# Thirteen output pairs of the input projection formed from seven block products, their weight sums on GpSimd, and the convolution's input moved through DRAM

## The chip, the core and the metric

The kernel runs on one core of a Trainium2 chip. A core has a matrix engine (TensorE, "PE" in the profile; the loading of its weights is "PEld"), a vector engine (VectorE, "DVE"), a scalar engine (ScalarE, "ACT"), a general engine (GpSimd, "POOL") and a queue engine (SyncE, "SP") that here only issues DMAs. Each engine executes its own instructions in the order in which they stand in its program, and waits on semaphores for the others. TensorE accumulates in PSUM, which GpSimd's operations in this kernel never touch; all else lies in SBUF or in DRAM.

The metric is the device time of one launch in microseconds (us): the median of several runs. Lower is better.

## The reference

The reference is one layer of a hybrid block on 1024 tokens of width 1024, all in float32. After an RMS norm, one wide projection gives the inputs of a gated unit (a convolution branch), of attention, and of two gates:

```python
h = rms_norm(x, norm1_g[l])
z = h @ w_in[l]
glu_in, q, k, v, gate_logits = jnp.split(z, SPLITS, axis=-1)
a_val, a_gate = jnp.split(glu_in, 2, axis=-1)
a = a_val * jax.nn.sigmoid(a_gate)
a = causal_depthwise_conv(a, conv_w[l], conv_b[l])      # 31 taps, each channel alone
a = jax.nn.silu(rms_norm(a, conv_norm_g[l]))
y_a = a @ w_conv_out[l]
...                                                     # dilated attention, 16 heads of 64 -> y_b
g_a, g_b = jnp.split(jax.nn.sigmoid(gate_logits + gate_b[l]), 2, axis=-1)
x = x + (g_a * y_a + g_b * y_b) @ w_out[l]
h = rms_norm(x, norm2_g[l])
u = causal_depthwise_conv(h @ w_up[l], ffn_conv_w[l], ffn_conv_b[l])
u_val, u_gate = jnp.split(u, 2, axis=-1)
x = x + (jax.nn.silu(u_gate) * u_val) @ w_down[l]       # d_ff 2816
```

The parts that this case is about are the four column groups of `z` called `a_val`, `a_gate`, `g_a` and `g_b`, each 1024 channels wide, and the 31-tap convolution.

## The kernel before, in words

**Precision.** A float32 product is made from three products of shortened numbers: every operand is split into a high part (rounded by a ScalarE copy) and a low part (what is left, a VectorE subtraction), and high x high, high x low and low x high are summed in PSUM. So each block product stands as three matmuls of 128 x 128 by 128 x 512. The helper `split` (L76 to L79) does it; the weights go through `wsplit` and `wpiece`.

**First stage.** The 1024 x 1024 tokens are normed, turned by TensorE and kept in SBUF in two halves of 512 tokens, as high and low parts (`hT`). Then come, in program text, (1) the gated unit: for each of eight tiles of 128 channels a gate product and a value product (`gemm_ch`, L115, 48 matmuls each), a sigmoid on ScalarE, a multiplication on VectorE (L445) whose result goes into one of ten padded SBUF rows `apad`; (2) the projections q, k and v, six groups of eight token tiles (`gemm_tok`, L120, 24 matmuls each); (3) the convolution (`conv_branch`, L450): 31 VectorE operations over 128 x 1024 for each of eight channel tiles, from `apad` to `cacc`. No table sets the order of this stage: a scheduler places the instructions of each engine from its own estimate of time. It starts the convolution as soon as the first channel tile exists, two channel tiles in turn, and lets it fill VectorE all through the stage. VectorE's other work (low parts, norms of q and k) is placed between.

**Attention.** Sixteen heads, each in eight slots. Here the order of PE, DVE and ACT is written out by hand (`manual_schedule`): scores, a VectorE minimum and mask (L592), an exponential on ScalarE (L597), a scaling of the row on GpSimd (L601), transposes (L607), a split into high and low parts, and the weighted sum. Between these, TensorE is given side work in steps of three matmuls: the sixteen gate tiles and the eight tiles of `w_conv_out` (`side_steps`), of which `FILL` says how many steps each of the eight slots takes, and `COVER` how many are done before attention starts, while the convolution is normed. VectorE forms the low parts of that side work in L163.

**Rest.** Output projections and merging, then the up projection of the feed-forward part, whose value and gate tiles are already formed together from seven block products instead of eight (`product`, L846, with the weight sums on VectorE), then the down projection.

## Time and profile before

| | |
|---|---|
| time, median of 3 runs | 1762.45 us (1762.37 to 1762.9) |
| span of the profiled execution, first to last instruction | 1761.6 us, 0.85 us under that median |
| busy: PE, PEld | 1749.1 us, 1454.3 us |
| busy: DVE, ACT, POOL | 1329.3 us, 771.7 us, 185.9 us |
| first token tiles turned and split | 0 to about 42 us |
| gated unit's products | 41.6 to 193.9 us |
| q, k, v | 193.9 to 470.5 us |
| convolution on VectorE | 44.7 to 479.4 us |
| attention with side work | about 494 to 944 us |

The profile's own execution ran for a span of 1761.6 us; the page shows no other time for it. "Busy" is the time in which an engine had an instruction in work. A row of a group reads: line, engine, operation, output <- inputs, shapes, count, then busy time and the mean length of one, then the idle time just before them and what ended it. A row of a timeline reads: start, length, engine, line, operation, output <- inputs, and in brackets the idle time before it with its releaser. Lengths of neighbouring instructions on VectorE and TensorE overlap a little, since the next one starts before the last one has drained.

### The profile page before, as it was taken

How to read it: one execution, taken by the hardware profiler on the slowest of the kernel's cores; microseconds unless marked ns; L12 is line 12 of the kernel's file. 1: busy time of each engine (PE TensorE's matmuls, PEld its weight loads, DVE VectorE, ACT ScalarE, POOL GpSimd, SP SyncE). 2: the span in 40 equal slices, each digit the busy share in tenths (PEclk: the TensorE clock that was granted, in tenths of full speed). 3: DMA queues.
4: the chain of work that ended last, by engine and by line, in shares of the span. 5: the costliest groups of instructions: out<-in, count | busy, mean ns of one | idle time of the engine just before them, and what ended most of it. 6: DMA issues, size and time to landing. Idle time of an engine off the chain costs nothing.

```text
span 1761.6 us, 22662 instructions
## 1 busy us (share of the span) xinstructions
PE 1749.1 (99%) x8248; PEld 1454.3 (83%) x8248; DVE 1329.3 (75%) x1837; ACT 771.7 (44%) x1235; POOL 185.9 (11%) x193
## 2 busy tenths in 40 slices
PE   8999999999999999999999999999999999999999
PEld 6888888888888888888888888888888888888887
DVE  6999999999846666667655564687776777779863
ACT  6111132232256666667564343454544544534431
POOL 1000133034012222222210000000000000000000
PEclk9999999999999999999999999999999999999999
DMA  5111145344585655568446567532222222498851
GB/s 208 48 48 49 42 138 164 123 132 139 179 273 157 179 159 159 161 180 244 139 138 227 173 233 279 207 124 84 84 84 84 77 91 84 128 341 320 292 174 48
DMA packets 146530, 272.79 MB, mean 155 GB/s; under 512 B 11761, under 2 KB 61041, under 8 KB 146418
## 3 DMA queue, kind: packets, MB, share of 16 engines
q1 hardware_dynamic: 145264, 269.24, 47.2%
q10 hardware_dynamic: 1154, 2.10, 0.3%
q8 instruction: 65, 1.06, 0.2%
q14 instruction: 47, 0.39, 0.1%
HBM read 197.90 MB, written 73.40 MB: 154 GB/s over the span
## 4 chain that ended last, share of the span: by engine, by line
PE 93%; DMA 4%; DVE 1%; issue 1%; ACT 1%; SPq 0%; ACTq 0%; DVEq 0%
PE dx L1118 6%; PE xz L850 6%; PE xz L851 6%; PE xz L852 6%; PE qkv L129 5%; PE qkv L127 5%; PE qkv L128 5%; PE dy L1118 4%; PE pp L607 3%; PE gate L110 3%; PE gate L112 3%; PE gate L111 3%; PE y L850 2%; PE y L851 2%; PE y L852 2%; PE o L622 2%
## 5 line engine op out<-in xcount | busy, mean ns | idle before, releaser
L461 DVE SCALAR_TENSOR_TENSOR cacc<-apad,pk,cacc 128x1024 f32<-128x1024 f32 x240 | 299.7, 1288 | 0.7
L79 DVE TENSOR_TENSOR pl<-pp,ph 128x512 fp32r<-128x512 f32 x192 | 100.8, 553 | 88.1 <-ACT ph L78 87.9
L127 PE MATMUL qkv<-hi_qkv,hT 128*128 128x512 f32 x384 | 151.8, 396 | 0.0
L129 PE MATMUL qkv<-hi_qkv,hT 128*128 128x512 f32 x384 | 150.2, 391 | 0.0
L128 PE MATMUL qkv<-lo_qkv,hT 128*128 128x512 f32 x384 | 149.3, 389 | 0.0
L78 ACT ACTIVATE ph<-pp 128x512 fp32r<-128x512 f32 x192 | 87.1, 488 | 121.0 <-PE pp L607 120.3
L592 DVE CUSTOM_DVE_ANT_0 p<-s,m 128x128 f32<-128x128 f32 (+7 forms) x128 | 96.5, 754 | 53.3 <-PE s L588 41.4
L601 POOL TENSOR_SCALAR p<-p,st 128x128 f32<-128x128 f32 (+7 forms) x128 | 97.1, 758 | 315.7 <-DVE st L600 218.7
L1021 DVE SCALAR_TENSOR_TENSOR u<-u,pk 128x1023 f32<-128x1023 f32 x88 | 112.4, 1279 | 1.0 <-ACT u L1019 0.7
L103 POOL TENSOR_TENSOR rs<-ss,mhalf 128x8 f32<-128x8 f32 x32 | 75.0, 2348 | 337.6 <-DVE ss L102 337.6
L110 PE MATMUL gate<-hT,hi_gt 128*128 128x512 f32 x256 | 103.0, 402 | 0.0
L597 ACT ACTIVATE p<-p,st 128x128 f32<-128x128 f32 (+7 forms) x128 | 99.3, 775 | 5.5 <-DVE st L592 4.6
L111 PE MATMUL gate<-hT,hi_gt 128*128 128x512 f32 x256 | 100.3, 392 | 0.0
L112 PE MATMUL gate<-hT,lo_gt 128*128 128x512 f32 x256 | 100.1, 392 | 0.0
L129 PEld LDWEIGHTS qkv<-hi_qkv,hT 128*128 128x128 f32 x384 | 72.1, 188 | 15.3
L79 DVE TENSOR_TENSOR lo_uv<-raw_uv,hi_uv 128x1024 fp32r<-128x1024 f32 x20 | 24.5, 1226 | 79.5 <-ACT hi_uv L78 79.5
L128 PEld LDWEIGHTS qkv<-lo_qkv,hT 128*128 128x128 f32 x384 | 72.2, 188 | 14.3
L607 PE MATMUL pp<-ident,p 128*128 128x128 f32 x576 | 83.8, 272 | 0.0
L127 PEld LDWEIGHTS qkv<-hi_qkv,hT 128*128 128x128 f32 x384 | 72.2, 188 | 13.9
L607 PEld LDWEIGHTS pp<-ident,p 128*128 128x128 f32 x576 | 70.1, 140 | 15.3
L621 PE MATMUL o<-ph,v 128*128 128x512 f32 x192 | 74.8, 393 | 0.7 <-DVE op L633 0.7
L850 PE MATMUL xz<-blk_t,hi_s3g 128*128 128x512 f32 x176 | 68.6, 390 | 0.7 <-ACT xc L995 0.7
(309 smaller groups left out, 4638.8 us busy)
## 6 DMA issues: line engine op xcount, KB each, us to landing
wr<-w_down SPq DMA_DIRECT2D x45, 512.0 KB, 5.5
gr<-dff SPq DMA_DIRECT2D x62, 256.0 KB, 5.2
raw_qkv<-w_qkv SPq DMA_DIRECT2D x24, 512.0 KB, 3.8
dff<-u SPq DMA_DIRECT2D x22, 512.0 KB, 2.6
raw_uv<-w_up SPq DMA_DIRECT2D x21, 512.0 KB, 3.2
raw_ug<-w_up SPq DMA_DIRECT2D x20, 512.0 KB, 3.2
dv<-v SPq DMA_DIRECT2D x16, 512.0 KB, 3.2
raw_gt<-w_ch SPq DMA_DIRECT2D x16, 512.0 KB, 5.2
```

The source lines that it names most:

```text
L110: pe.matmul(o, hi[:, k, :], ah[:, k, :], start=(k == 0), stop=False)
L111: pe.matmul(o, hi[:, k, :], al[:, k, :], start=False, stop=False)
L112: pe.matmul(o, lo[:, k, :], ah[:, k, :], start=False, stop=(k == KT - 1))
L127: pe.matmul(ps, ah, hi[:, k % 2, :], start=(k == 0), stop=False)
L128: pe.matmul(ps, ah, lo[:, k % 2, :], start=False, stop=False)
L129: pe.matmul(ps, al, hi[:, k % 2, :], start=False, stop=(k == KT - 1))
L461: dve.scalar_tensor_tensor(out=acc, in0=a[:, j : j + T], scalar=w(j), in1=acc, op0=ALU.mult, op1=ALU.add)
L607: pe.transpose(pp[:, qb * P : (qb + 1) * P], pts[qb][:, kt * P : (kt + 1) * P], ident)
L850: pe.matmul(o, wh[:, k, :], bh[:, k, :], start=(start and k == 0), stop=False, skip_group_check=not start)
L851: pe.matmul(o, wh[:, k, :], bl[:, k, :], start=False, stop=False, skip_group_check=not start)
L852: end = pe.matmul(o, wl[:, k, :], bh[:, k, :], start=False, stop=(k == 3), skip_group_check=not start)
L1118: pe.matmul(banks[n], a[:, c], b[:, d], start=(start and i == 0 and m == 0), stop=(stop and i == nf - 1 and m == 2), skip_group_check=True)
```

## The change

The gated unit's tiles 1 to 7 and six of the eight gate pairs (`GATES = 6`: columns g_a and g_b of the same tile) are formed as *pairs*: the value tile and the gate tile together are a 2 x 2 block product over two halves of the input width and two halves of the tokens, and are made from seven block products of 12 matmuls (`product`, now ahead of the stage) instead of eight. For that the tokens are needed in four more forms (`t1` to `t4`: sums and differences of the blocks, each 128 x 2048, split into high and low), and each pair's weights in four sums.

- The sums of the weights (`add_`, L409, four of 128 x 512 for each of the 13 pairs) are done by GpSimd. So are two additions of 128 x 2048 (`rebuilt`, L477) that put the blocks of the first token half together again from high and low part.
- Each pair's weights are now three pieces of 1024 columns and one of 512 that are split, where two pieces of 1024 were; each pair has three additions of PSUM halves on VectorE (L552, L558, L560).
- The gated unit's result goes through DRAM (`dain`) instead of staying in `apad`: the convolution has two `apad` and two `cacc` buffers, loads its input, and stores its result (`dacc`), from where it is loaded again to be normed (L712).
- The block `b12` of the tokens is spilled to DRAM and fetched again for q, k and v, since its room holds the results of the pairs in between.
- The side work left for `COVER` and attention is four gate tiles (6, 7, 14, 15) and `w_conv_out`; `FILL` is about halved to go with it, `COVER` stays.

```diff
-FILL = (1.5, 3.4, 1.8, 1.9, 1.6, 3.0, 2.1, 2.2)
+FILL = (0.7, 1.6, 0.9, 0.9, 0.8, 1.5, 1.0, 1.1)
+GATES = 6
...
-        for c in range(12):
+        left_over = [c for c in range(16) if c % 8 >= GATES]
+        turn = left_over[-4:]
+        for c in left_over[:-4]:
...
+        def pair_sums(i, v):
+            n, c, _, w2 = pairs[i]
+            g = stage(w2, f"{n}g{c}")
+            s = wp.tile([P, 1024], F32, tag="raw", bufs=4, name=f"{n}s12_{c}")
+            a11, a12, a21, a22 = v[:, 0:512], v[:, 512:], g[:, 0:512], g[:, 512:]
+            s1, s2 = s[:, 0:512], s[:, 512:]
+            add_ = lambda o, a, b, op: pool.tensor_tensor(out=o, in0=a, in1=b, op=op)
+            add_(s1, a21, a22, ALU.add)
+            add_(s2, s1, a11, ALU.subtract)
+            sw = wsplit(s, f"{n}s12_{c}")
+            add_(a21, a11, a21, ALU.subtract)
+            gw = wsplit(g, f"{n}s3g_{c}")
+            add_(a12, a12, s2, ALU.subtract)
+            return [four(t) for t in sw], [four(t) for t in gw], [four(t) for t in wsplit(a12, f"{n}s4_{c}")]
...
+            def rebuilt(n, k):
+                pool.tensor_tensor(out=plain[n], in0=h0[0][:, k : k + 4].bitcast(F32),
+                                   in1=h0[1][:, k : k + 4].bitcast(F32), op=ALU.add)
+            rebuilt("t2", 0)
...
+        dve.tensor_tensor(out=plain["t2"], in0=plain["t3"], in1=plain["t2"], op=add)
+        dve.tensor_tensor(out=plain["t4"], in0=plain["t4"], in1=plain["t2"], op=sub)
+        for n in ("t2", "t1", "t3", "t4"):
+            forms[n] = tform(n)
+            split(forms[n][:, 0], forms[n][:, 1], plain[n])
...
+            put(uv[:, t0], X, 0)
+            dve.tensor_tensor(out=uv[:, t0], in0=Z, in1=uv[:, t0], op=add)
+            product(X, sh[:, 4:8], sl[:, 4:8], *fb["t2"], False)
+            put(uv[:, t1], X, 0)
+            product(Y, sh[:, 0:4], sl[:, 0:4], *fb["t1"], True)
+            put(p5, Y, 1)
+            product(X, gh[:, 0:4], gl[:, 0:4], *fb["t3"], False)
+            dve.tensor_tensor(out=ug[:, t1], in0=X, in1=p5, op=add)
+            product(Y, *s4, *fb["b22"], False)
+            dve.tensor_tensor(out=uv[:, t1], in0=Y, in1=uv[:, t1], op=add)
+            product(X, gh[:, 4:8], gl[:, 4:8], *fb["t4"], False)
+            put(ug[:, t0], X, 1)
+            if kind == "u":
+                act.activation(ug, ug, AF.Sigmoid)
+                dve.tensor_tensor(out=uv, in0=uv, in1=ug, op=ALU.mult)
+                sp.dma_start(dain[c], uv)
...
-            else:
-                gp = big_ps(f"glug_{c}")
-                gemm_ch(gp, wsecond[0] if c == 1 else wpiece(w_ch[8 + c], f"g{c}"), hT)
-                act.activation(sg, gp, AF.Sigmoid)
-                vp = big_ps(f"gluv_{c}")
-                gemm_ch(vp, wsecond[1] if c == 1 else wpiece(w_ch[c], f"v{c}"), hT)
-                dve.tensor_tensor(out=a[:, CW - 1 :], in0=vp, in1=sg, op=ALU.mult)
...
-                acc = p1.tile([P, CW - 1 + T], F32, tag="apad", bufs=10, name=f"cacc_{c}")[:, 0:T]
-                a = apad[c]
+                a = p1.tile([P, CW - 1 + T], F32, tag="apad", bufs=2, name=f"apad_{c}")
+                pool.memset(a[:, : CW - 1], 0.0)
+                sp.dma_start(a[:, CW - 1 :], dain[c])
+                acc = p1.tile([P, T], F32, tag="cacc", bufs=2, name=f"cacc_{c}")
...
+            sp.dma_start(ct, dacc[c])
             dve.tensor_tensor(out=ct, in0=ct, in1=sqacc, op=ALU.mult)
```

How the instructions stand now, at three places. First GpSimd's queue while the first tokens are normed (`st` is the statistic of one token tile, raised to the power -1/2 here; `mhalf` holds that exponent). Before:

```order
L103 TENSOR_TENSOR st_214<-st_214,mhalf 128x1
L431 MEMSET apad_829 128x30
L431 MEMSET apad_944 128x30
L103 TENSOR_TENSOR st_214<-st_214,mhalf 128x1
L431 MEMSET apad_1059 128x30
```

Now (`raw_uv` and `raw_ug` are the loaded weights of a pair, `us` its sums):

```order
L104 TENSOR_TENSOR st_226<-st_226,mhalf 128x1 x4
L477 TENSOR_TENSOR sums<-hT_220,hT_221 128x2048
L104 TENSOR_TENSOR st_226<-st_226,mhalf 128x1
L409 TENSOR_TENSOR us_1_590<-raw_ug_588 128x512
L409 TENSOR_TENSOR us_1_590<-us_1_590,raw_uv_408 128x512
L409 TENSOR_TENSOR raw_ug_588<-raw_uv_408,raw_ug_588 128x512
L104 TENSOR_TENSOR st_226<-st_226,mhalf 128x1 x3
L477 TENSOR_TENSOR t_sum<-hT_220,hT_221 128x2048
```

The statistics of token tiles 4 to 7 now stand behind one addition of 128 x 2048 and three of the first pair's sums.

Second, VectorE in the middle of the stage (`cacc` is the convolution's sum). Before, between two products of the gated unit:

```order
L461 SCALAR_TENSOR_TENSOR cacc_3502<-apad_496,pk,cacc_3502 128x1024
L445 TENSOR_TENSOR apad_714<-gluv_773,sg_716 128x1024
L461 SCALAR_TENSOR_TENSOR cacc_3469<-apad_489,pk,cacc_3469 128x1024
L79 TENSOR_TENSOR lo_v_1007<-raw_v_1004,hi_v_1006 128x1024
L461 SCALAR_TENSOR_TENSOR cacc_3502<-apad_496,pk,cacc_3502 128x1024
```

Now, between two pairs:

```order
L80 TENSOR_TENSOR lo_uv_1017<-raw_uv_1014,hi_uv_1016 128x1024
L603 SCALAR_TENSOR_TENSOR cacc_4299<-apad_4296,pk,cacc_4299 128x1024
L80 TENSOR_TENSOR lo_us_5_1051<-us_5_1047,hi_us_5_1050 128x1024
L603 SCALAR_TENSOR_TENSOR cacc_4336<-apad_4333,pk,cacc_4336 128x1024
L560 TENSOR_TENSOR uring<-uy_u_942,uring 128x512
L603 SCALAR_TENSOR_TENSOR cacc_4299<-apad_4296,pk,cacc_4299 128x1024
L80 TENSOR_TENSOR lo_us3g_1056<-raw_ug_1045,hi_us3g_1055 128x1024
L565 TENSOR_TENSOR uring<-uring 128x1024
L558 TENSOR_TENSOR uring<-uxz_898,up_u_943 128x512
```

Operations of the pair (low parts of weights, additions of PSUM halves) stand between single steps of the convolution, so each of them comes after those steps in VectorE's order.

Third, where the convolution ends on VectorE, seen from the last piece of the last weights of q, k and v (`lo_qkv_3`; `ql`, `qn` and `ss` belong to the norms of q and k, `v_0` is the first of the last eight token tiles, all of which need that piece). Before:

```order
L79 TENSOR_TENSOR lo_qkv_3_3081<-raw_qkv_3_3078,hi_qkv_3_3080 128x1024
L79 TENSOR_TENSOR ql_4_3010<-qt_4_3004,qh_4_3009 128x512
L461 SCALAR_TENSOR_TENSOR cacc_3712<-apad_1174,pk,cacc_3712 128x1024
L79 TENSOR_TENSOR ql_5_3055<-qt_5_3049,qh_5_3054 128x512
L461 SCALAR_TENSOR_TENSOR cacc_3677<-apad_1059,pk,cacc_3677 128x1024
L488 TENSOR_TENSOR qn_6_3002<-qkv_6_2970,rs_4_6_2997 128x512
L102 TENSOR_SCALAR ss_4_7_3041<-ss_4_7_3041 128x8
L461 SCALAR_TENSOR_TENSOR cacc_3712<-apad_1174,pk,cacc_3712 128x1024
```

Now:

```order
L80 TENSOR_TENSOR lo_qkv_3_3908<-raw_qkv_3_3905,hi_qkv_3_3907 128x1024
L80 TENSOR_TENSOR ql_5_3882<-qt_5_3876,qh_5_3881 128x512
L603 SCALAR_TENSOR_TENSOR cacc_4564<-apad_4561,pk,cacc_4564 128x1024
L103 TENSOR_SCALAR ss_4_7_3868<-ss_4_7_3868 128x8
L80 TENSOR_TENSOR ql_6_3946<-qt_6_3940,qh_6_3945 128x512
L603 SCALAR_TENSOR_TENSOR cacc_4564<-apad_4561,pk,cacc_4564 128x1024
L629 TENSOR_TENSOR qn_7_3874<-qkv_7_3842,rs_4_7_3869 128x512
L603 SCALAR_TENSOR_TENSOR cacc_4564<-apad_4561,pk,cacc_4564 128x1024
L80 TENSOR_TENSOR v_0_3936<-qkv_0_3911,v_0_3936 128x8x64
L610 TENSOR_TENSOR sqacc<-sqacc,apad_4561 128x1024
```

Before, 25 of the convolution's steps stood behind this weight piece, the last of them behind the eighth of these token tiles. Now three do, all ahead of the first tile. On TensorE 147 of the 192 matmuls of the last eight tiles stand from the first use of that piece on.

220 lines of the change are left out of this document (150 added, 70 removed).

## Prediction

> **What bounds the kernel now.** I read the page's busy times, its slices and the shares of the chain first, and then the busy times of two stretches: the gated unit with q, k, v (42 to 480 us) and eight heads of attention (535 to 735 us).
>
> ```profile
> PE 1749.1 (99%) x8248; PEld 1454.3 (83%) x8248; DVE 1329.3 (75%) x1837; ACT 771.7 (44%) x1235; POOL 185.9 (11%) x193
> DVE  6999999999846666667655564687776777779863
> PE 93%; DMA 4%; DVE 1%; issue 1%; ACT 1%; SPq 0%; ACTq 0%; DVEq 0%
> 42.00:480.00 438.00, 438.00 (x1994) 362.35 (x1994) 426.31 (x449) 101.81 (x139) 75.02 (x32) 1.00 0.34 106
> 535.00:735.00 200.00, 200.00 (x1103) 170.60 (x1101) 129.39 (x327) 123.59 (x277) 48.61 (x65) 1.00 0.59 165
> ```
>
> In the stretches the columns are the stretch, its sum, then busy time of PE, PEld, DVE, ACT and POOL, the granted clock, the DMA share and GB/s. TensorE never pauses in either, so fewer matmuls are time won, as long as the others keep up. The share of 75% for VectorE hides where that fails: in the first stretch, the one that the change rebuilds, VectorE is busy for 426.31 of 438 us. There two engines set the end together, and the question is on which side of that balance the change falls.
>
> **TensorE's gain.** A pair takes 84 matmuls where two tiles took 96, so 13 pairs save 156.
>
> ```profile
> L110 PE MATMUL glug<-hT,hi_g x112: 389/389/389, 41.6 to 182.4; 128*128 128x512 f32 x112
> L127 PE MATMUL qkv<-hi_qkv,hT x384: 387/389/481, 193.9 to 469.8; 128*128 128x512 f32 x192
> L129 PE MATMUL qkv<-hi_qkv,hT x384: 388/389/481, 194.4 to 470.2; 128*128 128x512 f32 x192
> ```
>
> The row of `glug` is one of six groups of 112 (three passes, gate and value): 672 matmuls from 41.6 to 193.9 us, 0.2266 us each. So 156 are worth **35.4 us**. The stage itself grows, since gate work moves into it from attention: 13 x 84 = 1092 matmuls stand where 672 were, 95.2 us more. Its last matmul ended near 470.5 us and would end at 565.7 us if TensorE never waited. Attention's side work shrinks by the other 130.6.
>
> **VectorE's own work.** The prices:
>
> ```profile
> L461 DVE SCALAR_TENSOR_TENSOR cacc<-apad,pk,cacc 128x1024 f32<-128x1024 f32 x240 | 299.7, 1288 | 0.7
> L445 DVE TENSOR_TENSOR apad<-gluv,sg 128x1024 f32<-128x1024 f32 x7 | 8.6, 1226 | 3.9 <-PE gluv L112 3.9
> L79 DVE TENSOR_TENSOR lo_v<-raw_v,hi_v 128x1024 fp32r<-128x1024 f32 x6 | 7.3, 1221 | 1.5 <-ACT hi_v L78 1.5
> L79 DVE TENSOR_TENSOR v<-qkv,v 128x512 fp32r<-128x512 f32 x16 | 10.9, 697 | 3.3 <-ACT v L78 3.1
> L163 DVE TENSOR_TENSOR lo_gt<-raw_gt,hi_gt 128x512 fp32r<-128x512 f32 x8 | 5.2, 687 | 0.0
> 209.03 1.22 DVE L469 TENSOR_TENSOR sqacc<-sqacc,csq 128x1024 f32<-128x1024 f32 x1
> 210.17 1.29 DVE L461 SCALAR_TENSOR_TENSOR cacc<-apad,pk,cacc 128x1024 f32<-128x1024 f32 x1
> 475.49 3.93 DVE L461 SCALAR_TENSOR_TENSOR cacc<-apad,pk,cacc 128x1024 f32<-128x1024 f32 x3
> ```
>
> Gone ahead of the convolution's last step: 14 low parts of gated weights (17.1 us), seven multiplications (8.6), ten low parts of gate weights (6.9) and seven splits of `v` that now stand behind it (4.9): 37.5 us. New: low parts for 13 pairs, three of 1024 and one of 512 columns (13 x 4.35 = 56.6); 39 additions from PSUM at 0.68 (26.5); seven multiplications (8.6); eight differences of token tiles at 0.69 (5.5); and six operations over 2048 columns. Those have no row; another 512 columns cost 1.226 - 0.687 = 0.54, so 2.3 each, 13.8. Together 111.0, the balance +73.5. Recorded lengths overlap: the operation at 209.03 is 1.22 long, but the next starts 1.14 later, so I count 0.934 of them, 68.6 us. The convolution's last step before ends at 479.4; it would end at **548.0**.
>
> That is under 565.7, but the end is not where TensorE needs VectorE. By the third place of the order the last weight piece of q, k, v stands only three convolution steps and three operations of 512 (5.5 us) ahead of it, so at 542.5; and 147 matmuls (33.3 us) wait for it, which have to start at 532.4 to end at 565.7. VectorE is **10.1 us** late there with nothing else counted. Before, the piece came just in time, with 25 steps still behind it.
>
> **The sums on GpSimd.** 52 additions of 128 x 512 at GpSimd look free: it is busy for 75.02 of 438 us. Attention shows that they may not be.
>
> ```profile
> L601 POOL TENSOR_SCALAR p<-p,st 128x1024 f32<-128x1024 f32 x16 | 18.1, 1129 | 11.9 <-DVE st L600 11.5 <-PE pp L607 0.4
> L601 POOL TENSOR_SCALAR p<-p,st 128x512 f32<-128x512 f32 x16 | 11.4, 715 | 49.3 <-PE pp L607 47.7 <-DVE st L600 1.6
> L601 POOL TENSOR_SCALAR p<-p,st 128x128 f32<-128x128 f32 x16 | 6.0, 375 | 34.0 <-DVE st L600 29.4 <-PE pp L607 4.5
> 559.63 0.69 DVE L163 TENSOR_TENSOR lo_gt<-raw_gt,hi_gt 128x512 fp32r<-128x512 f32 x1
> 577.84 1.42 DVE L163 TENSOR_TENSOR lo_gt<-raw_gt,hi_gt 128x512 fp32r<-128x512 f32 x1
> 577.71 1.02 POOL L601 TENSOR_SCALAR p<-p,st 128x896 f32<-128x896 f32 x1 [2.26 <-DVE st L600]
> 555.04 1.10 DVE L163 TENSOR_TENSOR lo_gt<-raw_gt,hi_gt 128x512 fp32r<-128x512 f32 x1
> 554.47 1.13 POOL L601 TENSOR_SCALAR p<-p,st 128x1024 f32<-128x1024 f32 x1 [0.92 <-DVE st L600]
> 209.21 5.02 POOL L103 TENSOR_TENSOR rs<-ss,mhalf 128x8 f32<-128x8 f32 x2 [182.35 <-DVE ss L102]
> ```
>
> The same subtraction takes 0.69 us alone, 1.42 when GpSimd has just begun (GpSimd ends at 578.73, the subtraction 0.53 later) and 1.10 in the middle (GpSimd ends at 555.60, the subtraction 0.54 later). So a VectorE operation that reads two tiles from SBUF waits until GpSimd's running instruction is over. Convolution steps and low parts all read two; the additions from PSUM read one. A power over 128 x 8 (209.21) held up no step beside it; it reads far less.
>
> GpSimd has no row for an addition of two 128 x 512 tiles. With one input it takes 0.715, the lower bound. The rows give 0.84 ns for an element and 0.27 fixed; if the second input streams as well, 0.27 + 2 x 0.43 = 1.13, near what 1024 elements take. Less 0.15 of start, in which nothing was held, that is 0.565 to 1.0 us of hold. I take 1.0: a sum does read two tiles. Additions from PSUM are 26.5 of the some 228 us of twelve pairs, 12%, and can pass; so 52 x 0.88 x 1.0 = **46 us** (low: 26). The two additions of 128 x 2048 take by the same rows 2.0 (one stream) to 3.7, and four of the token tiles' powers stand behind one of them and three sums:
>
> ```profile
> 22.23 0.55 POOL L103 TENSOR_TENSOR st<-st,mhalf 128x1 f32<-128x1 f32 x1
> 24.87 1.29 DVE L313 SCALAR_TENSOR_TENSOR xs<-x,st,gb 128x1024 f32<-128x1024 f32 x1
> ```
>
> VectorE scales a tile 2 us after its power, so what delays the power delays it; I take 6 us for the pair of additions (3.7 to 7.2). Four us are given back, the idle time of L445, where VectorE waited for TensorE and won't; at most it is the 11.7 us of the first stretch. VectorE's lag at the weight piece: 10.1 + 46 + 6 - 4 = **58.1 us**, and TensorE ends q, k, v that much later. The bounds: 10.1 + 26 + 3.7 - 11.7 = 28, and 10.1 + 46 + 7.2 = 63.
>
> The Trainium skill, "GPSIMD Engine Reference", section "3.1 Elementwise — side-by-side cycle accounting", has 4497 ns for an addition of 2048 float32 on GpSimd against 2293 on VectorE; from it I estimate some 1.4 us for 512, which would make the sums 57 us and the time 11 us longer than mine. No run here shows that figure yet.
>
> **DRAM.** The nearest rows for the new transfers:
>
> ```profile
> dff<-u SPq DMA_DIRECT2D x22, 512.0 KB, 2.6
> raw_uv<-w_up SPq DMA_DIRECT2D x21, 512.0 KB, 3.2
> 497.23 9.17 DVE L568 TENSOR_TENSOR cacc<-cacc,sqacc 128x1024 f32<-128x1024 f32 x8
> 513.06 0.29 DVE L592 CUSTOM_DVE_ANT_0 p<-s,m 128x128 f32<-128x128 f32 x1 [6.66 <-DMA da<-cacc]
> ```
>
> A gated tile is stored and loaded in about 6 us, and a new one comes every 19 us (84 x 0.2266) while VectorE needs some 40 for one: hidden. `b12` is 2 MB, four such loads, 13 us; it is needed after four token tiles of q, 21.8 us: hidden by them, 13 if it were not. SP's queue holds weight loads behind these stores, but a pair ahead. At the norm it is different: the eight multiplications at 497.23 now need the stored sums back, through four buffers, and tiles 4 to 7 can only be fetched when tiles 0 to 3 have been stored as `da`, for which attention's first operation already waited 6.66 us. I take 4 us (0 if `COVER` hides it, 8 for one more store and load with its waits).
>
> **Attention.** Two rows of the chain, each the eight transposes of one place in a head, are eight heads apart:
>
> ```profile
> 531.94 0.87 PE pp L607 x8
> 730.65 0.87 PE pp L607 x8
> ```
>
> A head took 24.84 us. `FILL` sums to 8.5 steps in place of 17.5; nine steps of three matmuls are 6.1 us, leaving 18.7. In the stretch of 535 to 735, 8.05 heads, ACT was busy for 15.4 us in a head and VectorE for 16.1, up to 86% of 18.7. Fewer steps also cover less of each wait. I take 4 us for all heads (0 to 12).
>
> **The sum,** against the profile's own span of 1761.6: -35.4 + 58.1 + 4 + 4 gives 1792.3; the median of the runs is 0.85 above that span, so **1793 us**.
>
> **The rivals.** *The sums run beside VectorE* (a different operation, or GpSimd losing every race and waiting for gaps). For it: the power at 209.21 held up nothing. Against it: three rows of L163, and a VectorE without gaps. Then the lag is 10.1 - 4 = 6, and 1762.45 - 35.4 + 6 + 4 = **1737**. *The hold is real but short*, at its lower bound: 28 + 4 + 4 against 35.4 gives **1763**. *Attention becomes ACT's and VectorE's*: if heads fall only to 20.5 us (busy 16 plus the same 4.5 of waits as a chain of dependent steps would leave), 16 x 1.8 = 29 us come on top of the first rival, in place of its 4 us there: 1737 + 25 = **1762**; for it speaks the 86%, against it that side work is cut evenly over the slots. It decides once a head's dependent steps exceed 18.7 us.
>
> The Trainium skill, "SBUF — State Buffer", section "🔬 SBUF: two separate sides", calls the shared port pair an exclusive lock that is held for the whole instruction; by that rule the rival that hides the sums falls, and the L163 rows agree.
>
> **How the numbers follow.** Forecast 0.59 (own range 1755 to 1810: lag 28 with nothing added, lag 63 with 8 and 12), hidden sums 0.30, short hold 0.06, attention 0.05. About 0.2%, 3.5 us, is what a measurement of this kernel can tell from no change. Of the forecast nearly all is slower; the two cases around 1762 share 0.08 of no change. Faster takes the hidden sums and a little of the rest: 0.33, 0.08, 0.59. The range runs from 1738, which cuts the hidden sums in half, to 1810.
>
> **What would show it.** Right: TensorE idle between pairs, waiting for low parts or sums, periods of a pair near 22 us instead of 19; low parts of 1024 columns well over 1.22 and steps over 1.29 next to a GpSimd sum of about 1.1; q, k, v ending near 624. Wrong: VectorE's lengths unchanged and q, k, v ending by 575; or a head that stays over 20 us.

## The result, and the profile after

The changed kernel takes 1832.71 us (1832.1 to 1833.53) where the kernel before took 1762.41: a ratio of 1.040, 95% interval 1.038 to 1.041. It is slower by 70 us, and lies above the forecast range of 1738 to 1810. That it would be slower, and that VectorE would come late, was right; what attention and the way to it would lose was not.

The page of the changed kernel: its span, the busy times, TensorE's granted clock in slices, and the chain that ended last.

```profile
span 1830.3 us, 22688 instructions
PE 1747.9 (95%) x8092; PEld 1436.6 (78%) x8092; DVE 1431.7 (78%) x1904; ACT 818.5 (45%) x1285; POOL 304.3 (17%) x247
PEclk9999999999999989999999899999999999999999
PE 73%; DVE 15%; issue 5%; DMA 4%; ACT 2%; POOL 1%; SPq 0%; ACTq 0%; DVEq 0%; POOLq 0%
```

TensorE's share of the chain fell from 93% to 73%, VectorE's rose from 1% to 15%. TensorE has 156 matmuls fewer but is busy nearly as long as before (1749.1 us), in part because some of its matmuls now run at half clock (last section), and it idles for 82 us of the span, where it had idled for 12.5.

Four landmarks divide the run. The rows are from the views of single tiles: the last matmul of q, k and v, the first minimum of attention on VectorE, and the first matmul of the output projection.

```profile
L140 PE MATMUL qkv<-hi_qkv,hT x192: 387/389/481, 332.6 to 596.8; 128*128 128x512 f32 x192
L140 PE MATMUL qkv<-hi_qkv,b x96: 388/389/481, 366.5 to 618.5; 128*128 128x512 f32 x96
L737 DVE CUSTOM_DVE_ANT_0 p<-s,m x128: 274/754/1225, 676.0 to 988.3; 128x128 f32<-128x128 f32 x16, 128x256 f32<-128x256 f32 x16, 128x384 f32<-128x384 f32 x16, 128x512 f32<-128x512 f32 x16
L115 PE MATMUL yb<-oT,hi_ao x128: 389/389/796, 1009.8 to 1099.6; 128*128 128x512 f32 x128
```

| | before | changed | difference | of it matmuls | left over | forecast |
|---|---|---|---|---|---|---|
| to the last q, k, v matmul | 470.2 | 618.5 | +148.3 | +95.2 | **+53.1** | +58.1 |
| from there to the first minimum | 42.9 | 57.5 | +14.6 | 0 | **+14.6** | +4 |
| from there to the output projection | 431.3 | 333.8 | -97.5 | -130.6 | **+33.1** | +4 |
| from there to the end | 817.2 | 820.5 | +3.3 | 0 | **+3.3** | 0 |
| whole span | 1761.6 | 1830.3 | +68.7 | -35.4 | +104.1 | +66.1 |

"Of it matmuls" is the number of matmuls more or fewer times 0.2266 us; "left over" is what the stretch lost beyond them. So the lateness up to the last q, k, v matmul came out near its forecast, while attention cost eight times what was allowed for it.

What keeps TensorE waiting in the changed kernel, first from 40 to 620 us and then from there to the output projection (each row: who waits, for whom, us in all, how often, the longest; the longest rows of each):

```profile
PE uxz L123 <- DVE uring L552: 9.7, 6, 3.9
PE uy_t L125 <- DVE lo_ts L80: 4.9, 3, 3.5
PE qt L637 <- DVE qn L629: 4.7, 1, 4.7
PE tp L347 <- DVE sums L375: 4.2, 1, 4.2
PE uxz L125 <- DVE lo_uv L80: 3.7, 1, 3.7
...
PE s L732 <- DVE st L737: 16.6, 1, 16.6
PE yb L115 <- ACT hi_ao L79: 7.4, 1, 7.4
PE pp L752 <- POOL p L746: 5.1, 8, 1.5
```

The first five are waits for VectorE: the first two and the fifth in the stage of the pairs, the third where q, k, v begin, the fourth at the start. Of the last three, the first stands ahead of the first head; the kernel before has none of such length (its longest between 480 and 945 us is 0.7).

And GpSimd against VectorE, in the timeline of the changed kernel:

```profile
75.71 5.74 DVE L603 SCALAR_TENSOR_TENSOR cacc<-apad,pk,cacc 128x1024 f32<-128x1024 f32 x3
75.87 2.26 POOL L409 TENSOR_TENSOR us<-raw_ug 128x512 f32<-128x512 f32 x1 [4.32 <-DVE lo_us3g L80]
78.21 2.15 POOL L409 TENSOR_TENSOR us<-us,raw_uv 128x512 f32<-128x512 f32 x1
64.62 1.28 POOL L409 TENSOR_TENSOR us<-us,raw_uv 128x512 f32<-128x512 f32 x1
64.64 3.41 DVE L80 TENSOR_TENSOR ht<-t_sum,ht 128x2048 fp32r<-128x2048 f32 x1 [0.65 <-ACT ht L79]
17.50 4.57 DVE L530 TENSOR_TENSOR qkg<-pk 128x1 f32<-128x1 f32 x1
16.53 5.52 POOL L477 TENSOR_TENSOR sums<-hT,hT 128x2048 f32<-128x2048 f32 x1 [5.08 <-DVE hT L360]
```

Three convolution steps take 5.74 us where three took 3.93 before. The two engines go in turn: a sum of 2.26 us has waited some 1.1 for the step in progress, and runs in 1.1 to 1.28, during which the next step waits. The 1.28 is the fourth row: this sum began 0.02 us ahead of VectorE's next operation, which then took 3.41 us (its like take 2.28). An operation on one column takes 4.57 us, until the addition of 128 x 2048 is over at 22.05.

### The profile page after: what moved, and what is told of

It is laid out like the page before. It is cut to its first block, busy times and chain, and to the rows that moved or that the text cites. A ratio compares the mean times of both kernels' runs of the same rounds, so it can differ in the third digit from the quotient of the medians.

```text
span 1830.3 us, 22688 instructions
## 1 busy us (share of the span) xinstructions
PE 1747.9 (95%) x8092; PEld 1436.6 (78%) x8092; DVE 1431.7 (78%) x1904; ACT 818.5 (45%) x1285; POOL 304.3 (17%) x247
## 4 chain that ended last, share of the span: by engine, by line
PE 73%; DVE 15%; issue 5%; DMA 4%; ACT 2%; POOL 1%; SPq 0%; ACTq 0%; DVEq 0%; POOLq 0%
DVE cacc L603 7%; PE dx L1253 6%; PE xz L123 5%; PE xz L125 5%; PE xz L124 5%; PE dy L1253 4%; PE qkv L139 4%; PE qkv L140 4%; PE qkv L138 4%; PE pp L752 3%; PE y L123 2%; PE y L125 2%; PE y L124 2%; PE o L767 2%; PE o L766 2%
## 5 line engine op out<-in xcount | busy, mean ns | idle before, releaser
L603 DVE SCALAR_TENSOR_TENSOR cacc<-apad,pk,cacc 128x1024 f32<-128x1024 f32 x240 | 329.6, 1400 | 0.2
L752 PE MATMUL pp<-ident,p 128*128 128x128 f32 x576 | 89.9, 276 | 7.4 <-POOL p L746 5.1
L80 DVE TENSOR_TENSOR lo_uv<-raw_uv,hi_uv 128x1024 fp32r<-128x1024 f32 x27 | 36.1, 1337 | 77.7 <-ACT hi_uv L79 77.7
L732 PE MATMUL s<-kh,q 128*128 128x512 f32 (+1 forms) x192 | 66.3, 346 | 16.6 <-DVE st L737 16.6
L139 PE MATMUL qkv<-lo_qkv,hT 128*128 128x512 f32 x192 | 74.9, 390 | 0.9 <-DVE lo_qkv L80 0.9
L140 PE MATMUL qkv<-hi_qkv,hT 128*128 128x512 f32 x192 | 75.0, 391 | 0.0
L138 PE MATMUL qkv<-hi_qkv,hT 128*128 128x512 f32 x192 | 74.7, 396 | 0.0
L123 PE MATMUL xz<-blk_t,hi_s3g 128*128 128x512 f32 x176 | 68.6, 390 | 0.7 <-ACT xc L1130 0.7
L123 PE MATMUL xz<-h2left,hi_uv 128*128 128x512 f32 x176 | 68.6, 390 | 0.0
L124 PE MATMUL xz<-blk_t,hi_s3g 128*128 128x512 f32 x176 | 68.5, 389 | 0.0
L125 PE MATMUL xz<-h2left,lo_uv 128*128 128x512 f32 x176 | 68.5, 389 | 0.0
L124 PE MATMUL xz<-h2left,hi_uv 128*128 128x512 f32 x176 | 68.5, 389 | 0.0
L125 PE MATMUL xz<-blk_t,lo_s3g 128*128 128x512 f32 x176 | 68.5, 389 | 0.0
```

Source lines behind the costliest of these rows:

```text
L80: dve.tensor_tensor(out=lo, in0=src, in1=hi.bitcast(F32), op=ALU.subtract)
L123: pe.matmul(o, wh[:, k, :], bh[:, k, :], start=(start and k == 0), stop=False, skip_group_check=not start)
L124: pe.matmul(o, wh[:, k, :], bl[:, k, :], start=False, stop=False, skip_group_check=not start)
L125: end = pe.matmul(o, wl[:, k, :], bh[:, k, :], start=False, stop=(k == 3), skip_group_check=not start)
L138: pe.matmul(ps, ah, hi[:, k % 2, :], start=(k == 0), stop=False)
L139: pe.matmul(ps, ah, lo[:, k % 2, :], start=False, stop=False)
```

## The experiments

To see in which part of the stage time is lost, I take from the timeline of TensorE at a given moment the time minus 0.2266 us for each matmul of 512 columns begun so far, and call it the lost time. In the kernel before it is 18.9 us at 42 and still 18.9 at 200 us, where the gated unit is done. In the changed kernel it is 30.2 at 42 us, 61.8 at 300 us and 64.5 at 344 us, where the last matmul of the pairs begins. So of the 53.1 us, 11.3 come from the start, 34.3 from the stage of the pairs and 7.5 from q, k, v and the change-over to them. Not all of it is waiting: up to its last q, k, v matmul TensorE idles for 42.0 us, where the kernel before idled for 6.2; for the rest it works slower (last section).

All runs, with the median time, its ratio to the kernel before measured beside it, and the landmarks of the profiled execution:

| run | time | ratio, 95% interval | last q, k, v | first minimum | output projection |
|---|---|---|---|---|---|
| before (beside each run) | 1762 to 1765 | | 470.2 | 513.1 | 944.4 |
| changed | 1832.7 | 1.040 (1.038 to 1.041) | 618.5 | 676.0 | 1009.8 |
| sums on VectorE | 1809.6 | 1.026 (1.025 to 1.028) | 595.3 | 652.8 | 986.8 |
| no sums | 1799.6 | 1.021 (1.019 to 1.023) | 586.1 | 644.0 | 978.5 |
| start's additions on VectorE | 1833.1 | 1.039 (1.037 to 1.041) | 618.1 | 675.3 | 1011.4 |
| four tiles kept | 1820.0 | 1.032 (1.031 to 1.034) | 611.7 | 664.6 | 997.9 |
| all on VectorE, four tiles kept | 1796.9 | 1.019 (1.018 to 1.021) | 587.3 | 640.4 | 974.4 |
| TensorE kept busy | 1835.8 | 1.041 (1.039 to 1.042) | 619.5 | 677.2 | 1013.8 |
| four gate pairs | 1795.6 | 1.018 (1.017 to 1.020) | 549.0 | 607.5 | 972.1 |
| longer tail | 1802.1 | 1.022 (1.020 to 1.023) | 588.6 | 641.7 | 979.4 |
| shorter cover | 1798.9 | 1.020 (1.018 to 1.022) | 588.5 | 633.2 | 975.7 |
| gated pairs alone | 1841.0 | 1.045 (1.043 to 1.047) | 490.5 | 585.2 | 1019.3 |
| before, half the side work per head | 1782.6 | 1.011 (1.010 to 1.013) | 469.8 | 512.6 | 963.4 |
| before, no tail | 1778.8 | 1.008 (1.007 to 1.010) | 469.8 | 512.4 | 955.9 |

### Do the sums hold up VectorE?

Two theories: GpSimd's sums take VectorE's time, as the three rows of attention had suggested; or VectorE is late by its own new work and the sums run beside it. One run moves the sums, one leaves them out.

```diff
-            add_ = lambda o, a, b, op: pool.tensor_tensor(out=o, in0=a, in1=b, op=op)
+            add_ = lambda o, a, b, op: dve.tensor_tensor(out=o, in0=a, in1=b, op=op)
```

> The 52 additions of weights are done by VectorE instead of GpSimd, nothing else is changed. Theory H (a running addition on GpSimd holds up VectorE): each costs VectorE 0.64 us of its own in place of a hold of 1.1 or more, so 33 us come and at least 50 go; q, k, v end some 10 to 25 us earlier than at 618.7, the total is 1808 to 1823 us. Rival O (the sums ran beside VectorE, which is late by its own new work and its order): VectorE gets 33 us more, the total is about 1866 us.

```diff
-            s = wp.tile([P, 1024], F32, tag="raw", bufs=4, name=f"{n}s12_{c}")
...
-            sw = wsplit(s, f"{n}s12_{c}")
-            add_(a21, a11, a21, ALU.subtract)
+            sw = wsplit(g, f"{n}s12_{c}")
             gw = wsplit(g, f"{n}s3g_{c}")
-            add_(a12, a12, s2, ALU.subtract)
-            return [four(t) for t in sw], [four(t) for t in gw], [four(t) for t in wsplit(a12, f"{n}s4_{c}")]
+            return [four(t) for t in sw], [four(t) for t in gw], [four(t) for t in wsplit(v[:, 512:], f"{n}s4_{c}")]
```

> The 52 additions of weights are left out: the split pieces are loaded weights as they are, so the pairs' results are not those of the reference; matmuls, low parts and transfers keep their number and size. Theory H: VectorE loses the 45 us by which its steps and low parts are longer now than before; q, k, v end near 572 us, the convolution's steps are back at 1.29 us, the total is 1780 to 1790 us. Rival O: q, k, v end within 5 us of 618.7, the total stays at 1828 to 1833 us.

Moved to VectorE, the sums made the kernel 23 us faster although VectorE had 52 operations more; left out, which also takes away the wait for the sums to be made, 33 us faster. The hold is shown. Its size is in VectorE's groups up to 640 us, first of the changed kernel and then without sums:

```profile
L603 DVE SCALAR_TENSOR_TENSOR cacc<-apad,pk,cacc 128x1024 f32<-128x1024 f32 x240 | 329.6, 1400 | 0.2
L80 DVE TENSOR_TENSOR lo_us<-raw_uv,hi_us 128x512 fp32r<-128x512 f32 x7 | 9.1, 1300 | 0.0
L80 DVE TENSOR_TENSOR lo_ts<-raw_tv,hi_ts 128x512 fp32r<-128x512 f32 x6 | 6.3, 1044 | 0.0
L552 DVE TENSOR_TENSOR uring<-uxz,uring 128x512 f32<-128x512 f32 x13 | 8.8, 677 | 0.0
```

```profile
L595 DVE SCALAR_TENSOR_TENSOR cacc<-apad,pk,cacc 128x1024 f32<-128x1024 f32 x240 | 299.6, 1275 | 0.2
L80 DVE TENSOR_TENSOR lo_us<-raw_uv,hi_us 128x512 fp32r<-128x512 f32 x7 | 4.8, 685 | 0.6 <-ACT hi_us L79 0.6
L80 DVE TENSOR_TENSOR lo_ts<-raw_tv,hi_ts 128x512 fp32r<-128x512 f32 x6 | 4.1, 686 | 3.5 <-ACT hi_ts L79 3.5
L544 DVE TENSOR_TENSOR uring<-uxz,uring 128x512 f32<-128x512 f32 x13 | 8.9, 682 | 1.0 <-PE uxz L125 1.0
```

The steps are 30.0 us longer in all, the two groups of low parts 6.5, some smaller groups 4: 41 us, 0.78 for a sum. The additions from PSUM (last row of each) do not change, as forecast. Without sums the lost time goes from 30.2 at 42 us to only 31.7 at 300: TensorE runs through all pairs with waits of 0.2 us. With the sums on VectorE it reaches 41.0. So of the 41 us that VectorE loses, 32 reach TensorE at the end of q, k, v (618.5 against 586.1).

But the run without sums missed its expectation, its total by 10 us: q, k, v end at 586 and not 572. What remains there (20.7 us over the matmuls' own time) is the start and the change-over, which no sum causes. TensorE still waits 5.3 us for a normed q tile (`qn`) when it comes to q, k, v; the weight pieces and the first four token tiles arrive there at the end of VectorE's queue. What in that order could be changed was not tried.

### The two additions at the start

```diff
-                pool.tensor_tensor(out=plain[n], in0=h0[0][:, k : k + 4].bitcast(F32),
+                dve.tensor_tensor(out=plain[n], in0=h0[0][:, k : k + 4].bitcast(F32),
```

> Only the two additions of 128 x 2048 at the start move from GpSimd to VectorE. Theory H (they hold VectorE at its busiest: an operation of 0.15 us took 4.57 and one of 1.22 took 4.33 beside them, 7.5 us in all, and four powers stand behind them): VectorE pays 2 x 2.28 us itself, the lost time of TensorE at 42 us falls from 30.0 by 2 to 6 us, the total is 1826 to 1831 us. Rival S (the start is late by its own longer chain of turned and subtracted token tiles): the lost time at 42 us stays at 29 to 31 us, the total at 1831 to 1835 us.

1833.1 us, no change, and the lost time at 42 us is 30.2 as before: the rival, in size. But that does not make the additions free. TensorE's longest wait at the start of the changed kernel is for a subtraction that makes a new form and thereby frees the PSUM room of turned tiles (L375), and that subtraction stands on VectorE behind a low part that takes 4.33 us instead of 1.21, until the second addition on GpSimd is over:

```profile
42.76 1.94 PE L347 MATMUL tp<-ident,xs 128*128 128x128 f32 x8 [4.23 <-DVE sums L375]
37.67 4.33 DVE L80 TENSOR_TENSOR lo_uv<-raw_uv,hi_uv 128x1024 fp32r<-128x1024 f32 x1
41.93 0.68 DVE L375 TENSOR_TENSOR sums<-tp,sums 128x512 f32<-128x512 f32 x1
35.55 5.38 POOL L477 TENSOR_TENSOR t_sum<-hT,hT 128x2048 f32<-128x2048 f32 x1 [3.82 <-ACT t_sum L374]
```

With the additions on VectorE the waits up to 60 us are

```profile
PE tp L347 <- DVE sums L375: 5.4, 1, 5.4
PE tp L347 <- DVE st L103: 3.2, 1, 3.2
```

and the subtraction now stands behind VectorE's own addition (2.28 us), the statistic `st` behind a power that GpSimd reached only after three sums of weights. One wait took the place of another. Even with every addition on VectorE, those of the weights as well, the lost time at 42 us is 29.1. So the start's 11 us are work of the new forms, additions and subtractions together, whichever engine adds; no run took that work away, and how the 11 us divide stays open.

### The convolution through DRAM

```diff
-                acc = p1.tile([P, T], F32, tag="cacc", bufs=2, name=f"cacc_{c}")
+                acc = (p1 if c < 4 else p1k).tile([P, T], F32, tag="cacc", bufs=2 if c < 4 else 4, name=f"cacc_{c}")
...
-                sp.dma_start(dacc[c], acc)
+                if c < 4:
+                    sp.dma_start(dacc[c], acc)
+                accs.append(acc)
...
-            sp.dma_start(ct, dacc[c])
+            if c < 4:
+                sp.dma_start(ct, dacc[c])
```

Here `p1k` is a second pool, and `ct` is `accs[c]` for tiles 4 to 7.

> Convolution tiles 4 to 7 stay in SBUF until they are normed; tiles 0 to 3 still go through DRAM, into buffers that are free early. Theory B (what the first attention head waits for after q, k, v is the reloading of tiles 4 to 7 behind the stores of tiles 0 to 3): the first minimum comes 43 us after the last q, k, v matmul instead of 57, TensorE's idle stretch of 16.6 us is gone or under 4, the total is 1815 to 1820 us. Rival C (there is too little side work to cover the norm, whatever the transfers): the gap stays at 53 to 58 us, the total within 3 us of 1833.

The total is what theory B said, 1820.0, but not for its reason alone: the gap to the first minimum went from 57.5 to 52.9 us, not to 43, and 7 us were won ahead of it: TensorE's waits of 4.7 us for `qn` and 0.9 for `lo_qkv` are gone in this run, why was not looked into. The idle stretch is 12.0 us instead of 16.6. In the changed kernel VectorE had waited 10.8 us for the reloads, the longest in

```profile
661.44 1.23 DVE L713 TENSOR_TENSOR cn<-cn,sqacc 128x1024 f32<-128x1024 f32 x1 [6.90 <-DMA cn<-dacc]
```

What holds up the first minimum now is in VectorE's timeline of this run:

```profile
657.14 1.29 DVE L177 TENSOR_TENSOR aT<-raw_a,aT 128x512 fp32r<-128x512 f32 x2 [4.92 <-ACT aT L184]
660.88 1.29 DVE L177 TENSOR_TENSOR aT<-raw_a,aT 128x512 fp32r<-128x512 f32 x2 [2.45 <-ACT aT L184]
663.42 1.29 DVE L177 TENSOR_TENSOR lo_co<-raw_co,hi_co 128x512 fp32r<-128x512 f32 x2 [1.24 <-ACT hi_co L184]
664.63 0.28 DVE L745 CUSTOM_DVE_ANT_0 p<-s,m 128x128 f32<-128x128 f32 x1
```

With only four gate tiles left as side work, the order written by hand comes to the normed convolution's pieces (`aT`) and to the weights of `w_conv_out` before the first head, and they stand ahead of the first minimum on VectorE. Before, VectorE had nothing to do between the norm's eight multiplications (497.23 to 506.40) and the first minimum (513.06). TensorE's side work in the gap is gate matmuls in both kernels; what is new is that the later gate tiles bring the splitting of these pieces with them (`ask_conv` in `gate`). A run took 16 of the 20 steps away from that place, on top of the run with all additions on VectorE and four tiles kept:

```diff
-COVER = (24, 8, 20)
+COVER = (24, 8, 4)
```

> As the same run (1796.9 us), with 4 steps of side work in place of 20 between the norm of the convolution and the first head, which also moves the pieces of the normed convolution that VectorE splits (it waited 5.1 and 2.5 us for them ahead of the first minimum) behind it, and leaves 16 steps more for after the last head. Theory P (those pieces, not a want of steps, hold up the first head): the first minimum comes 43 to 47 us after the last q, k, v matmul instead of 53, the total is 1782 to 1790 us. Rival (fewer steps cover less): the gap stays at 50 us or more, TensorE idles longer there by what the 16 steps took (11 us), the total is 1794 to 1802 us.

The gap shrank to 44.7 us, as theory P said, and nothing was won (1798.9 against 1796.9): TensorE idles 14.6 us instead of 12.2, since the 16 steps (11 us) are missing there, and they come after the last head. So the pieces are what the first minimum waited for, but moving them together with the gate steps that bring them does not win the time back: the norm takes some 44 us all the same, and then has too few steps beside it. A run that keeps the steps and splits the pieces behind the first minimum was not made.

### All additions on VectorE and four tiles kept

This run joins the edits of three runs above.

> All additions on VectorE (the 52 sums and the two of 128 x 2048) and convolution tiles 4 to 7 kept in SBUF. If the three parts are separate: 1832.7 - 23 - 12.7 - 4 gives 1793 us, 1789 to 1798. If the gain of keeping tiles came from the order in which VectorE was late (its lag at the end of q, k, v fell by 7 us, the wait after it by 5), little of it is left once VectorE is less late: 1800 to 1806 us.

1796.9 us: the gains of 23 and 12.7 add up, the start's additions bring nothing. GpSimd now does no addition, and the lost time at 300 us is 34.0, near the 29.1 of 42 us. It is still 34 us slower than the kernel before, by the landmarks 21.9 up to the end of q, k, v, 10.2 in the gap, 33.3 in attention and 3.5 behind it, less the 35.4. Attention is the same 33 as in the changed kernel.

### Attention

The theory for these 33 us: a head has work that depends step by step on other engines, and side steps are worth their length only while they fill its waits. The last minimum of a head (128 x 1024) gives the period: before, it came at 526.55 in the first and at 899.00 in the last head, 24.83 us for each of 15 periods. In the changed kernel:

```profile
688.27 1.23 DVE L737 CUSTOM_DVE_ANT_0 p<-s,m 128x1024 f32<-128x1024 f32 x1 [0.42 <-PE s L733]
988.26 1.22 DVE L737 CUSTOM_DVE_ANT_0 p<-s,m 128x1024 f32<-128x1024 f32 x1 [0.33 <-PE s L733]
```

That is 20.0 us, not 18.7. To separate this from all else in the change, I gave the kernel before the halved table:

```diff
-FILL = (1.5, 3.4, 1.8, 1.9, 1.6, 3.0, 2.1, 2.2)
+FILL = (0.7, 1.6, 0.9, 0.9, 0.8, 1.5, 1.0, 1.1)
```

> The kernel before with the halved side work per slot of the change (8.5 steps for a head in place of 17.5); what is left over is done after the last head, so no work is dropped. Theory F (a head's dependent steps take some 20 us, and fewer side steps than that leave TensorE waiting): the period of a head falls from 24.84 to about 20 us, not 18.7, and the total is 15 to 30 us over 1762. Rival R (heads were slow in the changed kernel for another reason of its own, as its transfers or its late start): the period is 18.7 to 19.0 us, the total within 5 us of 1762.

Its heads, in the same two rows:

```profile
523.90 1.23 DVE L592 CUSTOM_DVE_ANT_0 p<-s,m 128x1024 f32<-128x1024 f32 x1 [0.41 <-PE s L588]
821.67 1.23 DVE L592 CUSTOM_DVE_ANT_0 p<-s,m 128x1024 f32<-128x1024 f32 x1 [0.27 <-PE s L588]
```

19.85 us, and the total 1782.6: 20 us lost with not a matmul less. Theory F holds: heads with half the side work cost 19.5 us from the first minimum to the output projection (450.8 against 431.3) in a kernel that has nothing else of the change.

The other part is the end. Of 384 side steps (of three matmuls), 52 were left after the last head before; in the changed kernel 4 are.

```diff
-FILL = (1.5, 3.4, 1.8, 1.9, 1.6, 3.0, 2.1, 2.2)
+FILL = (1.8, 4.0, 2.1, 2.2, 1.9, 3.5, 2.5, 2.5)
```

> The kernel before with 20.5 steps of side work for a head in place of 17.5, so that 4 steps instead of 52 are left after the last head; no work is dropped. Theory T (the change also lost the side work behind the last head, which had covered the way from the last weighted sum to the output projection): TensorE idles 7 us before the output projection and its clock halves for some 10 us after, the total is 1770 to 1776 us. Rival (that idle stretch belongs to the changed kernel, whose last head is late): no idle stretch over 2 us there, the total is 1760 to 1765 us.

The waits of this run around the last head:

```profile
PE yb L110 <- ACT hi_ao L78: 7.4, 1, 7.4
PE pp L607 <- DVE pl L79: 1.1, 1, 1.1
```

The kernel before, without its tail, has the idle stretch of 7.4 us that the changed kernel has. It cost 14 us in all (1778.8 against 1764.6 measured beside it); by the landmarks 12.2 ahead of the output projection and 4.2 behind it. The idle stretch came as theory T said, the total 2.8 us above its 1770 to 1776. Both losses together, 19.5 and 16.4, are 36 us; the changed kernel lost 33.1 and 3.3 there. Attention's share is thus accounted for in size, by two runs of the kernel before, each with one table changed; they were not joined in one run.

With all additions on VectorE and four tiles kept I tried to give the tail some steps back:

```diff
-FILL = (0.7, 1.6, 0.9, 0.9, 0.8, 1.5, 1.0, 1.1)
+FILL = (0.6, 1.4, 0.8, 0.8, 0.7, 1.3, 0.9, 1.0)
```

> As the run with all additions on VectorE and tiles 4 to 7 kept (1796.9 us), with 7.5 side steps for a head instead of 8.5, so that about 20 are left after the last head. Theory T: the idle stretch of 7.3 us before the output projection is gone, heads lose some 2 to 5 us in all, the total is 1788 to 1793 us. Rival (the steps are worth the same everywhere): the total stays at 1795 to 1799 us.

1802.1 us, 5 us slower, against both expectations. The idle stretch stayed:

```profile
970.74 0.39 PE L117 MATMUL ya<-aT,lo_co 128*128 128x512 f32 x1
979.44 0.79 PE L115 MATMUL yb<-oT,hi_ao 128*128 128x512 f32 x1 [7.90 <-ACT hi_ao L79]
```

The slots behind the last head take four steps each (`rate = ... else 4`), six of them 24; so 20 steps are used up ahead of the last weighted sum, and none is left for the way behind it. The run with the shorter cover also has 20 steps there, and its wait is 7.8 us. A head got 0.22 us shorter (19.82 against 20.04) for one step of 0.68 us less, so the heads lost some 7 us.

### Fewer gate pairs, and none

The first of two runs starts from the one with all additions on VectorE and four tiles kept:

```diff
-FILL = (0.7, 1.6, 0.9, 0.9, 0.8, 1.5, 1.0, 1.1)
-GATES = 6
+FILL = (1.0, 2.2, 1.2, 1.2, 1.1, 2.0, 1.4, 1.4)
+GATES = 4
```

> As the run with all additions on VectorE and tiles 4 to 7 kept, but with four gate pairs instead of six: 24 matmuls more (5.4 us), 128 steps of gate work more as side work (11.5 steps for a head, 20 after the last head). Theory F and B (attention and its start lose for want of side work that does not need the convolution): a head takes 22.0 us or less than 0.4 over 24.84 - 6 x 0.68 = 20.8, TensorE's idle stretch at the first head is under 5 us and that before the output projection under 2, attention wins back 15 to 25 us; but VectorE, with 38 us less of TensorE's time to hide in and 20 us less work, is 18 us later: 1785 to 1800 us. Rival: the idle stretches stay at 12 and 7 us, the total is 1805 to 1815 us.

1795.6 us, inside the expected range, but not clear of the run it starts from (the fastest single run with six took 1796.4, the slowest with four 1796.7), and the parts are others than expected: the way from the first minimum to the output projection has 364.6 us, 20 over what its matmuls ask (431.3 - 87.0), so 13 were won back; the wait for `hi_ao` stayed at 7.9. The gap ahead of the first head grew to 58.5 us, since the convolution's last steps (574 us) now end behind q, k, v, and TensorE waits 6.6 us for its sum of squares.

The other end of the scale, from the changed kernel itself:

```diff
-FILL = (0.7, 1.6, 0.9, 0.9, 0.8, 1.5, 1.0, 1.1)
-GATES = 6
+FILL = (1.5, 3.4, 1.8, 1.9, 1.6, 3.0, 2.1, 2.2)
+GATES = 0
```

> The changed kernel with GATES = 0 and the side work per slot of the kernel before: only the seven gated-unit pairs are left of the change, all sixteen gate tiles are side work again. If the loss sits in attention's missing side work, it is gone here, 84 matmuls (19 us) are saved and the start costs 11: 1755 to 1770 us. If VectorE is the bound (it loses 36 us of low parts and additions and some 24 us of holds with the six gate pairs, but TensorE loses 114 us of work to hide it in), the convolution ends near 526 us instead of 479, TensorE idles some 35 us ahead of the first head, attention takes the 431 us it took before, and the total is 1805 to 1825 us.

```profile
PE pss L694 <- DVE sqacc L610: 33.6, 1, 33.6
PE s L732 <- DVE st L737: 10.9, 1, 10.9
```

1841 us, the slowest of all, and 16 above the upper end of what I had expected for a bound on VectorE. Attention takes 434.1 us, as before the change (431.3), so its loss is gone; but TensorE waits 33.6 us for the convolution's sum of squares, because VectorE got the pairs' work and TensorE lost the gate products that had hidden it. The convolution ended at 543 us, later than the 526 I had worked out. The two halves of the change need each other: gate pairs give VectorE time and take attention's side work away.

### The half clock

In the changed kernel the granted clock is 0.5 after each longer idle stretch (last section). To see what that costs ahead of the first head:

```diff
+                if at == 2:
+                    idle = bank_ps("idle")
+                    for _ in range(60):
+                        pe.matmul(idle, tiles[0][0][:, 0:P], tiles[0][1][:, 0:512], start=True, stop=True)
```

> The changed kernel with 60 further matmuls of 512 columns (13.6 us, into a PSUM bank that nobody reads) where TensorE idled for 16.6 us before the third score of the first head. Theory K (after an idle stretch of more than some 3.5 us the granted clock is 0.5 for 3.4 to 17 us, which costs matmul time): the half clock from 675 to 692 us is gone, the matmuls after the wait go at 0.23 instead of 0.43 us, the total falls by 4 to 8 us to 1825 to 1829 us although 60 matmuls are added. Rival N (the half clock comes from something else, or what it slows is waited for anyway): the total is within 2 us of 1832.7, or longer.

The idle stretch fell from 16.6 to 3.2 us and the half clock of 17.1 us to two of 3.4, but the time did not fall (1835.8). That is rival N's total. Of the 17.1 us the first 11.5 had been idle anyway, which leaves 5.6 at half speed, an estimate of 2.8 us; why the added matmuls made the kernel 3 us slower was not looked into. What the half clocks in the stage of the pairs cost was not measured by itself.

## Why the prediction was right or wrong

**TensorE's gain** stands: the 156 matmuls are gone, and outside the stretches of half clock one begins every 0.2266 us as before. It is the only gain, and 104 us of lost time stand against it.

**VectorE's own work** was near. The convolution was to end at 548.0 us with no sums counted; without sums its last step ends at 553.2. But the 10.1 us that I had put at the last weight piece did not arise there: the changed kernel's wait for `lo_qkv` is 0.9 us. Without sums TensorE runs through the pairs and waits 5.3 us for `qn` where q, k, v begin. So that term agrees in size alone.

**The sums on GpSimd** were right in kind and near in size: 46 us of hold forecast, 41 measured on VectorE; 1.13 us for a sum, 1.1 to 1.28 measured. That all of the hold would reach TensorE was not right: 32 us did. The rival that hides the sums had 0.30 and is refuted by the first two runs (its 1737 us also left out the 4 us of the gap that the forecast has). The page's figure of the Trainium skill (GPSIMD Engine Reference, section 3.1), from which I had estimated 1.4 us for a sum and 57 us in all, was the worse price for the whole (41 measured), and as good as mine for one sum (1.28 at the most).

**The start** was mis-sized. I had 6 us, for two additions at up to 3.7 us; they take 5.4 to 5.5, and 4.46 from the end of VectorE's operation in progress (17.59) to their own (22.05). The start lost 11.3, and moving the additions to VectorE won nothing, since VectorE then has them to do.

In sum the lag was 53.1 for 58.1, and that nearness is in part luck: without the sums 20.7 us of it remain, for which the forecast had 12.1 (10.1, 6 and -4), and the sums themselves cost 32 there for 46. The step that failed is **attention**, and with it the gap ahead of it:

- "Nine steps of three matmuls are 6.1 us, leaving 18.7" took every removed step as time won, with 4 us for all heads. Heads took 20.0, and the kernel before with the same table took 19.85. I had looked at the busy time of ACT and VectorE, up to 86%, and concluded that they were no bound; but a head is a chain of short waits across four engines, and the share of busy time does not show its length. The rival that named it (20.5 us, 29 us in all) had 0.05, and was tied to the case in which the sums are hidden: it should have stood on top of the forecast.
- The tail was not looked at. Of the 192 steps that left the side work, 144 were taken from the heads and 48 from the tail, and the prediction counted the 48 as pure gain. The run without a tail lost 16 us by its landmarks.
- **The gap** was to cost 4 us, 8 at most; it cost 14.6. The reloading that I had priced accounts for some 4.6 of it (57.5 to 52.9). The rest, 10 us, goes with the order: the gate steps in the gap now bring the splitting of the normed convolution with them, and the first minimum waits for it. The run with the shorter cover took 8 us off the gap but idled instead, so that this rest can be won back is not shown. The profile of before could not show the new order, but the list of side work could: 192 steps less 64 of gates are all of `w_conv_out`.

Heads, tail and gap lost 51.0 us for a forecast of 8; with the 5 us by which the lag was smaller than forecast, a net loss of 30.7 us became 68.7.

## What to carry to other kernels

Work that covers waits in a stage is worth its own length only while the stage stays bound by it; before taking it away, count how much is left for each wait, in the body and behind its last turn, and try the kernel before with just that much less, which costs one line. That an engine is idle most of the time does not make work on it free: what counts is whether its instructions stop the engine that is the bound. Here a cut in TensorE's work could pay only where the other engines had that much time to spare in the same stage, and moving work between stages moved the shortage too.

## What the runs showed of the hardware

GpSimd's additions and VectorE's operations with two inputs from SBUF alternate, instruction by instruction: neither starves. A sum costs VectorE 0.78 us on average, more than the 0.61 after which VectorE begins its next operation when it does the sum itself (0.69 recorded). So such an addition was cheaper on the engine that was to be relieved. Operations with one input from PSUM were not held (0.677 us with sums, 0.682 without). One input from SBUF can be enough, though: the convolution's first step for a tile, which reads one tile and two columns, took 1.78 us in the two cases where it began beside a sum, and 0.81 in the other six.

TensorE's clock, which I had not expected to matter: in the changed kernel's TensorE timeline,

```profile
110.40 0.50 PE L125 MATMUL uxz<-hT,lo_uv 128*128 128x512 f32 x1 [3.74 <-DVE lo_uv L80]
110.74 0.40 PE L123 MATMUL uxz<-hT,hi_uv 128*128 128x512 f32 x1
112.34 0.63 PE L123 MATMUL uxz<-hT,hi_uv 128*128 128x512 f32 x1
112.77 0.63 PE L124 MATMUL uxz<-hT,hi_uv 128*128 128x512 f32 x1
115.54 0.39 PE L125 MATMUL uxz<-hT,lo_uv 128*128 128x512 f32 x1
```

after 3.74 us of idling the matmuls start 0.43 us apart instead of 0.23, from about 111.9 to 115.3. Each of the seven idle stretches of 3.5 us or more up to the output projection is followed by a granted clock of 0.5, for 3.4, 6.8, 10.2 (after 7.4 us of idling) or 17.1 us (after 16.6), that is 1, 2, 3 or 5 times 3.41 us; in the longer ones part of the time is still idle. Two shorter stretches, of 2.3 and 2.6 us, are followed by it too, while one of 3.3 us in the run with TensorE kept busy is not. The Trainium skill, "TensorE: Matmul & The Clock Gate", section "What's actually happening", has the half clock after an idle window of some 3.4 us, with which most of these agree. For the five such windows of 3.4 us between 100 and 370 us, half of each is an estimate of 8.5 us within the 53.1; with the two at the start, less the idle time in them, it is some 12. From 1009.8 us, where the output projection begins, the clock is halved until 1016.4: an estimate of 3.3 us, the loss behind that landmark.
